# An encoder layer's up projection: one 512-column matmul in place of two of 256 in five of its seven products, with PSUM in pairs of banks

## The chip, the core and the metric

The kernel runs on one core of one Trainium2 chip. The metric is the device time of one execution in microseconds (us), the median of several runs. Engines are named as in the profile: PE is TensorE's matmul, PEld its weight load, DVE is VectorE, ACT is ScalarE, POOL is GpSimd, SP is SyncE. PSUM is the memory that PE writes; it has eight banks of 512 float32 values in each of 128 partitions.

## The reference

One layer of a streaming encoder on 512 tokens of width 2048, all in float32:

```python
h = rms_norm(x, pre_mix_g)
z = h @ w_in                        # q, k, v, u
a = chunked_attention(q, k, v, rel_bias)
p = multiscale_pool(u, pool_w, pool_scale)
x = x + rms_norm(concat([a, p]) @ w_o, post_mix_g)
h = rms_norm(x, pre_ffn_g)
up = causal_dwconv(h @ w_up, conv_w, conv_b)          # 2048 -> 2 * 5632, 3 taps
y = (gelu(up[..., :5632]) * up[..., 5632:]) @ w_down
x = x + rms_norm(y, post_ffn_g)
```

The change touches only `h @ w_up`.

## The kernel before

**Products in three parts.** A float32 factor is split into a high part, rounded to the type that PE multiplies in one pass, and a low part, the rest. ACT writes the high part (L135), DVE the low part (L136). A product of two split factors is three matmuls that add up in PSUM: `mm3` (L150 to L153) issues high by high (L151), high by low (L152) and low by high (L153).

**The up projection.** The columns of `w_up` are taken in 44 blocks k of 256 (two times 128), and each block's product with h is made by Winograd's form of Strassen's scheme: seven half-size products, numbered 1 to 7, in place of eight. One product (k, i) is 1024 deep and 256 tokens wide: `seven` (L853) runs over eight slices `kb` of 128 and issues three matmuls for each, 24 in all. The stationary operand is a 128x128 piece of w's factor (tiles `wfh` and `wfl`), the moving operand 256 columns of h's factor i, whose high and low part lie beside each other in one tile (`gT` for factors 1, 2, 5 and 3, `h` for 7, 4 and 6).

**The results of a block.** Products 1 and 2 share one PSUM bank (`q12`, half a bank each), 5 and 7 another (`q57`), 3 and 4 a third (`q34`), 6 has its own (`q6`). `half_bank` (L815) takes the bank that has been free longest from the list `spare`, and `done_bank` gives it back. `keep_six` (L829) follows product 6: ACT copies product 1 out (L844), DVE adds 6, 5 and 7, and 2 to it in the SBUF tile z (L845 to L850). `keep_all` (L1077) follows product 3: DVE adds both halves of `q34` into z in one instruction (L1080), and then the three taps of the convolution run on z (`taps`: ACT L1052, DVE L1053 and L1054), for an even block with the gelu (`gate`), for an odd one with the product of the two (`product`, DVE L1070). The tile z has two buffers.

**The order.** PE's order is the program's; the other engines' order is chosen by a scheduler. `Factors.order` (L700 to L712) lists the products. From block 5 to 42 a block's row is (k, 4), (k, 1), (k, 2), (k-1, 6), (k, 5), (k, 7), (k-1, 3): product 3 of a block ends the row of the next block, and product 4 of the block after that follows at once. Blocks 2 and 3 go together, and their last products (2, 6), (3, 6), (2, 3), (3, 3) stand directly before (4, 4). `Factors.get` splits each factor four products ahead; its tiles are those of the product that has just ended, so ACT's split waits for PE there.

After the up projection the down projection runs (`p` tiles, matmuls of 512 columns).

Of the kernel before, what the change touches and what calls it, by code (L numbers as in the profile page):

```python
# [9 lines left out]
F32 = mybir.dt.float32  # L10
F32R = mybir.dt.float32r
AF = mybir.ActivationFunctionType
# [3 lines left out]
P = 128  # L16
S = 512
# [11 lines left out]
WARM = 9  # L29
NU = KF // 2  # L30
EARLY = 5
CU = 4
AHEAD = 3
T = S // 2
# [42 lines left out]
def encoder_layer(ctx: ExitStack, tc: tile.TileContext, x, xT, vecs, rel, post_mix, post_ffn,  # L77
# [7 lines left out]
    nc = tc.nc  # L85
# [5 lines left out]
    mixing = ctx.enter_context(ExitStack())  # L91
    acc = mixing.enter_context(tc.tile_pool(name="acc", bufs=1))
    psum = ctx.enter_context(tc.tile_pool(name="psum", bufs=1, space=bass.MemoryType.PSUM))
    dram = ctx.enter_context(tc.tile_pool(name="dram", bufs=1, space=bass.MemoryType.DRAM))

    cycle = list(range(8))

    def bank(name, at=None):
        if at is None:
            at = cycle.pop(0)  # L100
            cycle.append(at)
        return psum.tile([P, 512], F32, tag=f"ps{at}", bufs=1, name=name)

    def acc8(name, which, dt=F32):
        return acc.tile([P, 2048], dt, tag="acc" + which, bufs=2, name=name)
# [44 lines left out]
    def mm3(ps, l, r, first, last):  # L150
        nc.tensor.matmul(ps, l[0], r[0], start=first, stop=False)  # L151
        nc.tensor.matmul(ps, l[0], r[1], start=False, stop=False)  # L152
        nc.tensor.matmul(ps, l[1], r[0], start=False, stop=last)  # L153
# [8 lines left out]
    def part(w, *idx):  # L162
        return tuple(v[(slice(None),) + idx] for v in w)
# [34 lines left out]
    for h in range(1, HEADS):  # L198
        q, k = qk_specs(h)
# [51 lines left out]
    for kb in range(KD):  # L251
        i, o = divmod(kb, 8)
        nc.sync.dma_start(xt[kb // 4][:, kb % 4, :], xT[kb * P:(kb + 1) * P, :])
        for what in "qk":
            if kb in chunks:
                raw, hi, lo = first[f"{what}0_{i}"]
# [5 lines left out]
        for what in "qk":  # L262
            _, hi, lo = first[f"{what}0_{i}"]
# [13 lines left out]
    with tc.tile_pool(name="p1", bufs=2, reuse_waits="tile") as p1:  # L277
# [209 lines left out]
        for g in range(4):  # L487
            hi, lo = (v[g].rearrange("p (a b) -> p a b", a=2) for v in (first_h, first_l))
# [32 lines left out]
        def at(f, kb, sl=slice(None)):  # L521
            return tuple(f[kb // 4][:, half, kb % 4, sl] for half in range(2))
# [56 lines left out]

    NC = (NU - 2) // CU  # L580
    H, C = S // 2, D // 2
    gd = [[dram.tile([P, CU, 2, H], F32, name=f"gd{c}_{i}") for i in range(2)] for c in range(NC)]
    gd_last = [dram.tile([P, 2, S], F32, name=f"gd{u}") for u in (NU - 2, NU - 1)]
# [109 lines left out]
    class Factors:  # L693
# [3 lines left out]
        def __init__(self):  # L697
            n = 2 * NU

            self.order = [(k, i) for k in range(EARLY) for i in (1, 2)]  # L700
            self.order += [(0, 5), (0, 7), (1, 5), (0, 6), (1, 7), (1, 6), (0, 3), (1, 3), (0, 4), (1, 4)]
            self.order += [(j, i) for i in (4, 7, 5, 6, 3) for j in (2, 3)]
            for k in range(EARLY - 1, n):
                late = [(k - 1, 6), (k - 1, 3)]
                if k < EARLY:
                    o = [(k, 4), (k, 7), (k, 5)]
# [6 lines left out]
            self.last = n - 1  # L713
            self.alone = *range(EARLY), n - 1
            self.raw, self.made, self.loaded, self.used = {}, [], 0, 0
# [6 lines left out]
        def source(self, k, i):  # L722
# [5 lines left out]
            if i == 7:  # L728
                return "v" if k < EARLY else "y"
            return "w" if i == 4 and k in self.alone else "x"  # L730
# [31 lines left out]
        def make(self, k, i):  # L762
            early, what = k < EARLY, self.source(k, i)
            v = self.raw[k, what]
# [41 lines left out]
    def flat(v):  # L806
        return v.rearrange("p a b -> p (a b)")

    p3, factors = None, Factors()
    banks, gates, zs, spare = {}, {}, {}, []  # L810

    def raw_x(name):
        return p3.tile([P, 1024], F32, tag="x", bufs=3, name=name)
# [1 line left out]
    def half_bank(k, i):  # L815
        tag = {5: "57", 7: "57", 1: "12", 2: "12", 6: "6", 3: "34", 4: "34"}[i]
        if (k, i) == (3, 6):
            return banks[2, "6"][0], slice(T, S)
        if (k, tag) not in banks:
            n = spare.pop(0)  # L820
            banks[k, tag] = bank(f"q{tag}_{k}", n), n
        return banks[k, tag][0], slice(T, S) if i in (7, 2, 4) else slice(0, T)

    def done_bank(k, tag):
        ps, n = banks.pop((k, tag))
        spare.append(n)
        return ps

    def keep_six(k, z=None):  # L829

        z = flat(new_z()) if z is None else z
        if k == 0:
            factors.held["r"].append((k, "six"))
            factors.raw[k, "six"] = z
        if k == 3:
            q6 = done_bank(2, "6")[:, T:]
        elif k == 2:
            q6 = banks[2, "6"][0]
        else:
            q6 = done_bank(k, "6")  # L840
        q57, q12 = (done_bank(k, n) for n in ("57", "12"))
        v2 = z[:, 3 * T:]
        for v in (v2, z[:, :T]):
            nc.scalar.activation(v, q12[:, :T], AF.Copy)  # L844
        nc.vector.tensor_add(v2, q6[:, :T], v2)  # L845
        nc.vector.tensor_add(z[:, T:3 * T].rearrange("p (a b) -> p a b", a=2),
                             q57.rearrange("p (a b) -> p a b", a=2),
                             v2[:, None, :].to_broadcast([P, 2, T]))
        nc.vector.tensor_add(v2, q57[:, :T], z[:, 2 * T:3 * T])
        nc.vector.tensor_add(z[:, :T], q12[:, T:], z[:, :T])  # L850
        zs[k] = z

    def seven(k, i):  # L853
        w = factors.get()
        ps, half = half_bank(k, i)
        for kb in range(8):
            mm3(ps[:, half], part(w, kb), at(h_f[i], kb), kb == 0, kb == 7)

    m = [None] * NT
    for i, tag in ((7, "raw1"), (4, "wh")):  # L860
# [8 lines left out]
    with tc.tile_pool(name="p2", bufs=1, reuse_waits="tile") as p2:  # L869
# [113 lines left out]
        for n in (5, 3):  # L983
            B = new_banks(f"m{n}", 4 if n == 5 else 0)
            for cc in range(2):
                late = (lambda q: h0.append(next(turning))) if n == 3 else None
                h0, ps = [], [B[cc, t] for t in range(2)]
# [17 lines left out]
        h_f = {1: gT[0][0], 2: gT[0][1], 5: gT[1][0], 3: gT[1][1]}  # L1005
        spare = [4, 5, 6, 7, 3]
# [8 lines left out]
        spare = [0, 1, 2]  # L1015
# [31 lines left out]
    p3 = phase.enter_context(tc.tile_pool(name="p3", bufs=2, reuse_waits="tile"))  # L1047
# [8 lines left out]
    def new_z():  # L1056
        return p3.tile([P, 2, S], F32, tag="z", name="z")
# [19 lines left out]
    def keep_all(k):  # L1077
        z = zs.pop(k)
        factors.raw.pop((k, "six"), None)
        nc.vector.tensor_add(z[:, T:3 * T], done_bank(k, "34"), z[:, T:3 * T])  # L1080
        z = z.rearrange("p (a b) -> p a b", a=2)
        u = k // 2
        if k % 2:
            product(u, gates.pop(u), z)
        else:
            gates[u] = gate(u, z)
# [28 lines left out]
    def next_first():  # L1115
# [2 lines left out]
        r = rights[0].send(i)  # L1118
        firsts.append((i, next(lefts), r))

    for k, i in rest:
        seven(k, i)
        if (k, i) == (end - 1, 3):
            next_first()
        if (k, i) == (2, 6):
            continue
        if i == 6:
            if k == 3:
                keep_six(2)
            keep_six(k)  # L1130
            if k == end:
                next_first()
        if i == (4 if k < 2 else 3):
            keep_all(k)
    cycle[:] = spare
    firsts = [(i, multiply(l, r)) for i, l, r in firsts]
    phase.close()

# [244 lines left out]
```

## Time and profile before

| | |
|---|---|
| median of 3 runs | 1920.13 us (1920.1 to 1920.24) |
| the profiled execution | 1921.21 us, of it span 1919.4 us |
| PE busy | 1890.6 us, 11898 matmuls |
| DVE busy | 1416.2 us |
| ACT busy | 949.9 us |
| granted TensorE clock, mean | 0.991 |

Times in the trace count from the start of the span. The attention and the output projection fill the span up to about 590 us, the up projection goes from there to about 1460 us, and the down projection takes the rest. A matmul's duration in the profile holds the time that its results take to drain, so those of neighbours overlap: the pace is the distance from start to start, or a stretch divided by the matmuls in it. A row of the timeline has start, duration, engine, line and tiles (written <- read), and in brackets how long the engine sat idle before it and for whom. A row of the windows has the stretch, its length, busy time with the number of instructions of each engine asked for, the granted clock as a share of full speed, the share of DMA and GB/s.

### The profile page before, as it was taken

How to read it: one execution, taken by the hardware profiler on the slowest of the kernel's cores; microseconds unless marked ns; L12 is line 12 of the kernel's file. 1: busy time of each engine (PE TensorE's matmuls, PEld its weight loads, DVE VectorE, ACT ScalarE, POOL GpSimd, SP SyncE). 2: the span in 40 equal slices, each digit the busy share in tenths (PEclk: the TensorE clock that was granted, in tenths of full speed). 3: DMA queues.
4: the chain of work that ended last, by engine and by line, in shares of the span. 5: the costliest groups of instructions: out<-in, count | busy, mean ns of one | idle time of the engine just before them, and what ended most of it. 6: DMA issues, size and time to landing. Idle time of an engine off the chain costs nothing.

```text
span 1919.4 us, 29449 instructions
## 1 busy us (share of the span) xinstructions
PE 1890.6 (98%) x11898; PEld 1719.5 (90%) x11898; DVE 1416.2 (74%) x1626; ACT 949.9 (49%) x1178; POOL 290.6 (15%) x383
## 2 busy tenths in 40 slices
PE   9999999999998999999999999999999899999998
PEld 7888888888888999999999999999998688888887
DVE  5554345686688677777777777777778899998877
ACT  6333233355487455445444454544545555565543
POOL 5000000000011121111111111111110112222211
PEclk9999999999999999999999999999999899999999
DMA  9747947667877876776766767667676779999998
GB/s 330 213 120 170 247 115 203 156 186 228 285 279 200 213 170 150 182 181 152 187 157 170 188 150 187 164 159 189 158 183 192 259 209 261 250 221 248 220 226 242
DMA packets 175529, 383.81 MB, mean 200 GB/s; under 512 B 11041, under 2 KB 62625, under 8 KB 172833
## 3 DMA queue, kind: packets, MB, share of 16 engines
q0 software_dynamic: 45472, 137.38, 38.5%
q1 hardware_dynamic: 129920, 244.55, 37.6%
q8 instruction: 93, 1.52, 0.3%
q14 instruction: 44, 0.35, 0.1%
HBM read 325.27 MB, written 90.18 MB: 216 GB/s over the span
## 4 chain that ended last, share of the span: by engine, by line
PE 92%; DVE 4%; DMA 2%; issue 1%; ACT 1%; SPq 0%; POOL 0%; POOLq 0%; DVEq 0%; ACTq 0%
PE q L153 16%; PE q L151 16%; PE q L152 16%; PE p L153 6%; PE p L152 6%; PE p L151 6%; PE m L152 2%; PE m L151 2%; PE m L153 2%; PE u L151 2%; PE v L152 2%; PE u L152 2%; PE v L151 2%; PE u L153 2%; PE v L153 2%; PE k L152 1%
## 5 line engine op out<-in xcount | busy, mean ns | idle before, releaser
L151 PE MATMUL q<-gT,wfh 128*128 128x256 f32 x1392 | 394.4, 283 | 0.0
L152 PE MATMUL q<-gT,wfh 128*128 128x256 f32 x1392 | 394.2, 283 | 0.0
L153 PE MATMUL q<-gT,wfl 128*128 128x256 f32 x1392 | 394.1, 283 | 0.0
L151 PE MATMUL q<-h,wfh 128*128 128x256 f32 x1056 | 300.7, 285 | 8.5 <-DVE z L845 7.2
L152 PE MATMUL q<-h,wfh 128*128 128x256 f32 x1056 | 300.6, 285 | 1.4 <-DVE h L136 1.4
L153 PE MATMUL q<-h,wfl 128*128 128x256 f32 x1056 | 300.7, 285 | 0.8 <-DVE wfl L136 0.8
L135 ACT ACTIVATE wfh<-wx 128x1024 fp32r<-128x1024 f32 x171 | 181.3, 1060 | 192.0 <-PE q L152 142.4
L152 PEld LDWEIGHTS q<-gT,wfh 128*128 128x128 f32 x1392 | 267.5, 192 | 0.2 <-DVE gT L136 0.2
L151 PEld LDWEIGHTS q<-gT,wfh 128*128 128x128 f32 x1392 | 267.5, 192 | 0.0
L153 PEld LDWEIGHTS q<-gT,wfl 128*128 128x128 f32 x1392 | 267.4, 192 | 0.0
L136 DVE TENSOR_TENSOR wfl<-wx,wfh 128x1024 fp32r<-128x1024 f32 x171 | 208.7, 1222 | 66.0 <-ACT wfh L135 65.8
L152 PE MATMUL p<-bl,ah 128*128 128x512 f32 x560 | 220.4, 394 | 4.4 <-DVE bl L136 4.4
L153 PE MATMUL p<-bh,al 128*128 128x512 f32 x560 | 220.4, 394 | 2.1 <-DVE al L136 2.1
L151 PE MATMUL p<-bh,ah 128*128 128x512 f32 x560 | 220.2, 393 | 1.8 <-ACT ah L135 1.8
L151 PEld LDWEIGHTS q<-h,wfh 128*128 128x128 f32 x1056 | 204.5, 194 | 8.9 <-DVE z L845 7.4
L152 PEld LDWEIGHTS q<-h,wfh 128*128 128x128 f32 x1056 | 204.4, 194 | 1.8 <-DVE h L136 1.8
L153 PEld LDWEIGHTS q<-h,wfl 128*128 128x128 f32 x1056 | 204.5, 194 | 1.0 <-DVE wfl L136 1.0
L135 ACT ACTIVATE bh<-b 128x2048 fp32r<-128x2048 f32 x70 | 133.3, 1915 | 76.8 <-DVE b L629 44.0
L136 DVE TENSOR_TENSOR bl<-b,bh 128x2048 fp32r<-128x2048 f32 x70 | 159.0, 2287 | 11.9 <-PE p L152 6.0
L760 POOL DMA_DIRECT2D wx<-in_w_up x90 | 79.6, 888 | 519.5 <-DVE wfl L136 440.6
L135 ACT ACTIVATE wfh<-wy 128x1024 fp32r<-128x1024 f32 x82 | 86.6, 1057 | 107.8 <-PE q L152 107.5
L136 DVE TENSOR_TENSOR wfl<-wy,wfh 128x1024 fp32r<-128x1024 f32 x82 | 100.3, 1223 | 48.4 <-ACT wfh L135 48.4
(417 smaller groups left out, 3729.6 us busy)
## 6 DMA issues: line engine op xcount, KB each, us to landing
wx<-in_w_up POOLq DMA_DIRECT2D x90, 512.0 KB, 6.3
b<-in_w_down SPq DMA_DIRECT2D x42, 1024.0 KB, 7.8
sum<-part POOLq DMA_DIRECT2D x70, 512.0 KB, 8.3
wx<-in_w_up SPq DMA_DIRECT2D x45, 512.0 KB, 5.9
wy<-in_w_up SPq DMA_DIRECT2D x44, 512.0 KB, 6.5
wz<-in_w_up SPq DMA_DIRECT2D x44, 512.0 KB, 5.2
wy<-in_w_up POOLq DMA_DIRECT2D x39, 512.0 KB, 6.1
wo_sum<-in_w_o POOLq DMA_DIRECT2D x16, 1024.0 KB, 11.2
```

The costliest lines, as they stand in the source:

```text
L135: rounded = nc.scalar.activation(hi, src, AF.Copy)
L136: nc.vector.tensor_sub(lo, src, f32(hi))
L151: nc.tensor.matmul(ps, l[0], r[0], start=first, stop=False)
L152: nc.tensor.matmul(ps, l[0], r[1], start=False, stop=False)
L153: nc.tensor.matmul(ps, l[1], r[0], start=False, stop=last)
L760: nc.gpsimd.dma_start(self.raw[k, what], self.block(k, m, kh), accum_op=ALU.add)
```

## The change

From block 4 on (`PAIRED = 4`), products 3 to 7 no longer use `mm3`. For each `kb` there is one matmul of w's high part with 512 moving columns, both parts of h's factor at once (now L910), which fills a whole bank: high by high in the first 256 columns, high by low in the last 256. A second matmul adds w's low part by h's high part to the first half (L909 for the last `kb`, where it goes ahead, else L912). So a product has 16 matmuls instead of 24, and its result is the sum of the two halves of its bank, which DVE has to add. Products 1 and 2 stay as they were.

A product then needs a whole bank. From (4, 4) on, PSUM holds bank 0 for `q12`, bank 1 for `q6`, and three pairs of banks: one pair for products 5 and 7, and two for 3 and 4, of which block k takes number `k % 2`. Nothing is taken from `spare` any more.

The steps behind the products become: `begin_z` (after product 2: an ACT copy L843 and a DVE add L844), `keep_pair` (after 5 and 7: an ACT copy L849 of 512 values into a tile t57, and a DVE add L850 of the other halves), `finish_six` (after 6: two DVE adds L856 from PSUM, and L857 and L859 within SBUF), and in `keep_all` two DVE adds L1140 of 512 values where there was one. For block 4 `begin_z` stands before the product (4, 4), since its `q12` lies in a bank that the pairs take.

```diff
+PAIRED = EARLY - 1
...
-            n = spare.pop(0)
+            n = k - 2 if tag == "34" and k in (2, 3) else spare[0]
+            spare.remove(n)
...
+    def pair_bank(k, i):
+        tag = "57" if i in (5, 7) else "34"
+        if (k, tag) not in banks:
+            n = 2 if tag == "57" else k % 2
+            banks[k, tag] = pairs.tile([P, 2, S], F32, tag=f"pair{n}", bufs=1, name=f"q{tag}_{k}")
+        return banks[k, tag][:, int(i in (7, 4)), :]
+
+    def begin_z(k):
+        z = zs[k] = flat(new_z())
+        q12 = banks.pop((k, "12"))[0]
+        nc.scalar.activation(z[:, 3 * T:], q12[:, :T], AF.Copy)
+        nc.vector.tensor_add(z[:, :T], q12[:, T:], z[:, 3 * T:])
+
+    def keep_pair(k):
+        q57 = banks.pop((k, "57"))
+        t57[k] = v = p3.tile([P, 2, T], F32, tag="t", bufs=1, name="t57")
+        nc.scalar.activation(v, q57[:, :, :T], AF.Copy)
+        nc.vector.tensor_add(v, q57[:, :, T:], v)
+
+    def finish_six(k):
+        z, q6, t = zs[k], banks.pop((k, "6")), t57.pop(k)
+        v2 = z[:, 3 * T:]
+        for half in range(2):
+            nc.vector.tensor_add(v2, q6[:, half * T:(half + 1) * T], v2)
+        nc.vector.tensor_add(z[:, T:3 * T].rearrange("p (a b) -> p a b", a=2), t,
+                             v2[:, None, :].to_broadcast([P, 2, T]))
+        nc.vector.tensor_add(v2, t[:, 0, :], z[:, 2 * T:3 * T])
...
         for kb in range(8):
-            mm3(ps[:, half], part(w, kb), at(h_f[i], kb), kb == 0, kb == 7)
+            hi, lo = part(w, kb)
+            if kb == 7:
+                nc.tensor.matmul(ps[:, :T], lo, at(h_f[i], kb)[0], start=False, stop=False)
+            nc.tensor.matmul(ps.rearrange("p (a b) -> p a b", a=2), hi, both(h_f[i], kb), start=kb == 0, stop=kb == 7)
+            if kb < 7:
+                nc.tensor.matmul(ps[:, :T], lo, at(h_f[i], kb)[0], start=False, stop=False)
...
-        nc.vector.tensor_add(z[:, T:3 * T], done_bank(k, "34"), z[:, T:3 * T])
+        if k < PAIRED:
+            nc.vector.tensor_add(z[:, T:3 * T], done_bank(k, "34"), z[:, T:3 * T])
+        else:
+            q34, v = banks.pop((k, "34")), z[:, T:3 * T].rearrange("p (a b) -> p a b", a=2)
+            for half in range(2):
+                nc.vector.tensor_add(v, q34[:, :, half * T:(half + 1) * T], v)
...
     for k, i in rest:
+        if k == PAIRED and pairs is None:
+            begin_z(k)
+            singles.close()
+            pairs = up_banks.enter_context(
+                tc.tile_pool(name="pairs", bufs=1, space=bass.MemoryType.PSUM, reuse_waits="tile"))
         seven(k, i)
```

How the order moves, at three places. First PE, at the seam of two rows of the list: the end of product 3 of block 18 and the start of product 4 of block 20 (`q34_18` and `q34_20` are the PSUM tiles of products 3 and 4 of these blocks; brackets name the engines whose counters the matmul waits on). Before:

```order
L151 MATMUL q34_18_8905<-gT11_4767,wfh_9190 128x256
L152 MATMUL q34_18_8905<-gT11_4767,wfh_9190 128x256
L153 MATMUL q34_18_8905<-gT11_4767,wfl_9191 128x256
L151 MATMUL q34_20_9361<-h40_5119,wfh_9218 128x256 [waits Activation_49]
L152 MATMUL q34_20_9361<-h40_5119,wfh_9218 128x256
L153 MATMUL q34_20_9361<-h40_5119,wfl_9219 128x256 [waits DVE_49]
```

Now:

```order
L910 MATMUL q34_18_8426<-gT11_4770,wfh_8667 128x512
L912 MATMUL q34_18_8426<-gT11_4770,wfl_8668 128x256
L909 MATMUL q34_18_8426<-gT11_4770,wfl_8668 128x256
L910 MATMUL q34_18_8426<-gT11_4770,wfh_8667 128x512
L910 MATMUL q34_20_8810<-h40_5122,wfh_8698 128x512 [waits DVE_49,PE_49,Activation_49]
L912 MATMUL q34_20_8810<-h40_5122,wfl_8699 128x256
```

Before, the first matmul of (20, 4) waits for its factor alone: ACT's high part on L151, DVE's low part on L153. Now it also waits, on DVE, for the second L1140 of block 18, which reads both banks of the pair that `q34_20` takes over.

Second DVE, at the same seam (`wfl` are splits of later factors, `z` the sums of block 18). Before:

```order
L136 TENSOR_TENSOR wfl_9258<-wy_9057,wfh_9257 128x1024 [waits DMAHW5_49,PE_49,Activation_49]
L136 TENSOR_TENSOR wfl_9290<-wz_9087,wfh_9289 128x1024 [waits DMAHW7_49,PE_49,Activation_49]
L1080 TENSOR_TENSOR z_9248<-q34_18_8905,z_9248 128x512 [waits DVE_49,PE_49]
L136 TENSOR_TENSOR wfl_9320<-wx_8799,wfh_9319 128x1024 [waits DMASW7_49,Activation_49]
L1053 SCALAR_TENSOR_TENSOR ca_9348<-z_9248,vec_71,ca_9348 128x511 [waits DMASW6_49,DMASW5_49,Activation_49]
```

Now:

```order
L144 TENSOR_TENSOR wfl_8727<-wy_8554,wfh_8726 128x1024 [waits DMAHW5_49,PE_49,Activation_49]
L144 TENSOR_TENSOR wfl_8751<-wz_8579,wfh_8750 128x1024 [waits DMAHW7_49,PE_49,Activation_49]
L850 TENSOR_TENSOR t57_8770<-q57_19_8731,t57_8770 128x512 [waits Activation_49]
L1140 TENSOR_TENSOR z_8501<-q34_18_8426,z_8501 128x512 [waits PE_49]
L1140 TENSOR_TENSOR z_8501<-q34_18_8426,z_8501 128x512 [waits DVE_49]
L144 TENSOR_TENSOR wfl_8776<-wx_8340,wfh_8775 128x1024 [waits DMASW7_49,Activation_49]
```

The addition of products 5 and 7 of block 19 (L850) has come in ahead of the two L1140, of which the second waits for the first.

Third DVE, around the last products of blocks 2 and 3, ahead of (4, 4) (`z_5758`, now `z_5761`, belongs to block 3). Before:

```order
L1080 TENSOR_TENSOR z_5758<-q34_3_5544,z_5758 128x512
L136 TENSOR_TENSOR wfl_5848<-wy_5637,wfh_5847 128x1024 [waits DMAHW1_49,PE_49,Activation_49]
L1053 SCALAR_TENSOR_TENSOR cb_5833<-z_5758,vec_71,cb_5833 128x511 [waits Activation_49]
L1053 SCALAR_TENSOR_TENSOR cb_5838<-z_5758,vec_71,cb_5838 128x511 [waits Activation_49]
L1054 SCALAR_TENSOR_TENSOR cb_5833<-z_5758,vec_71,cb_5833 128x510 [waits DVE_49]
L1054 SCALAR_TENSOR_TENSOR cb_5838<-z_5758,vec_71,cb_5838 128x510 [waits DVE_49]
L1070 TENSOR_TENSOR ca_5795<-ca_5795,cb_5833 128x512 [waits DVE_49]
L1070 TENSOR_TENSOR ca_5795<-ca_5795,cb_5838 128x512 [waits DVE_49]
```

Now:

```order
L1136 TENSOR_TENSOR z_5761<-q34_3_5547,z_5761 128x512
L1108 SCALAR_TENSOR_TENSOR cb_5836<-z_5761,vec_74,cb_5836 128x511 [waits Activation_49]
L1108 SCALAR_TENSOR_TENSOR cb_5841<-z_5761,vec_74,cb_5841 128x511 [waits Activation_49]
L1109 SCALAR_TENSOR_TENSOR cb_5836<-z_5761,vec_74,cb_5836 128x510 [waits DVE_49]
L1109 SCALAR_TENSOR_TENSOR cb_5841<-z_5761,vec_74,cb_5841 128x510 [waits DVE_49]
L1125 TENSOR_TENSOR ca_5798<-ca_5798,cb_5836 128x512 [waits DVE_49]
L1125 TENSOR_TENSOR ca_5798<-ca_5798,cb_5841 128x512 [waits DVE_49]
L844 TENSOR_TENSOR z_5848<-q12_4_5041,z_5848 128x256 [waits Activation_49]
```

`begin_z(4)` (L844) now stands behind the whole convolution of block 3, and the first matmul of (4, 4) waits for it; before, that matmul waited for L849 of block 2, which stands ahead of all these rows.

More of the change, by code (lines that the diff above doesn't have):

```diff
@@ L93, in encoder_layer, with upper @@
     psum = ctx.enter_context(tc.tile_pool(name="psum", bufs=1, space=bass.MemoryType.PSUM))
+    singles = ctx.enter_context(ExitStack())
+    def upper(name, stack):
+        return stack.enter_context(tc.tile_pool(name=name, bufs=1, space=bass.MemoryType.PSUM, reuse_waits="tile"))
+    upper_pool = upper("psb", singles)
     dram = ctx.enter_context(tc.tile_pool(name="dram", bufs=1, space=bass.MemoryType.DRAM))
@@ L101, in bank @@
             cycle.append(at)
-        return psum.tile([P, 512], F32, tag=f"ps{at}", bufs=1, name=name)
+        pool = psum if at < 2 else upper_pool
+        return pool.tile([P, 512], F32, tag=f"ps{at}", bufs=1, name=name)
     def acc8(name, which, dt=F32):
@@ L809, in encoder_layer @@
     p3, factors = None, Factors()
-    banks, gates, zs, spare = {}, {}, {}, []
+    banks, gates, zs, t57, spare, pairs = {}, {}, {}, {}, [], None
     def raw_x(name):
@@ L851, in keep_six, with both @@
         zs[k] = z
+    def both(f, kb):
+        return f[kb // 4][:, :, kb % 4, :]
     def seven(k, i):
         w = factors.get()
-        ps, half = half_bank(k, i)
-        for kb in range(8):
-            mm3(ps[:, half], part(w, kb), at(h_f[i], kb), kb == 0, kb == 7)
+        if k < PAIRED or i < 3:
+            if k > PAIRED and (k, "12") not in banks:
+                banks[k, "12"] = bank(f"q12_{k}", 0), 0
+            ps, half = half_bank(k, i)
+            for kb in range(8):
+                mm3(ps[:, half], part(w, kb), at(h_f[i], kb), kb == 0, kb == 7)
+            return
+        if i == 6:
+            ps = banks[k, "6"] = bank(f"q6_{k}", 1)
+        else:
+            ps = pair_bank(k, i)
+        for kb in range(8):
+            hi, lo = part(w, kb)
[4 more added lines that the diff above has]
+                nc.tensor.matmul(ps[:, :T], lo, at(h_f[i], kb)[0], start=False, stop=False)
     m = [None] * NT
@@ L1079, in keep_all @@
         factors.raw.pop((k, "six"), None)
-        nc.vector.tensor_add(z[:, T:3 * T], done_bank(k, "34"), z[:, T:3 * T])
+        if k < PAIRED:
+            nc.vector.tensor_add(z[:, T:3 * T], done_bank(k, "34"), z[:, T:3 * T])
+        else:
+            q34, v = banks.pop((k, "34")), z[:, T:3 * T].rearrange("p (a b) -> p a b", a=2)
+            for half in range(2):
+                nc.vector.tensor_add(v, q34[:, :, half * T:(half + 1) * T], v)
         z = z.rearrange("p (a b) -> p a b", a=2)
@@ L1119, in next_first @@
         firsts.append((i, next(lefts), r))
+    up_banks, done = ctx.enter_context(ExitStack()), {}
     for k, i in rest:
-        seven(k, i)
+        if k == PAIRED and pairs is None:
[3 more added lines that the diff above has]
+                tc.tile_pool(name="pairs", bufs=1, space=bass.MemoryType.PSUM, reuse_waits="tile"))
+        seven(k, i)
+        if k > PAIRED and i == 2:
+            begin_z(k)
+        done.setdefault(k, set()).add(i)
+        if k >= PAIRED and i in (5, 7) and {5, 7} <= done[k]:
+            keep_pair(k)
         if (k, i) == (end - 1, 3):
@@ L1129, in encoder_layer @@
                 keep_six(2)
-            keep_six(k)
+            if k < PAIRED:
+                keep_six(k)
+            else:
+                finish_six(k)
             if k == end:
@@ L1134, in encoder_layer @@
             keep_all(k)
-    cycle[:] = spare
+    up_banks.close()
+    upper_pool = upper("psb", ctx)
+    for n in range(2, 8):
+        bank("place", n)
+    cycle[:] = 4, 5, 0, 2, 3, 1, 6, 7
     firsts = [(i, multiply(l, r)) for i, l, r in firsts]
```

## The prediction

> **What bounds the kernel now.** I read the page's totals and its chain first, then the costliest groups, then windows and the timeline of the up projection.
>
> ```profile
> span 1919.4 us, 29449 instructions
> PE 1890.6 (98%) x11898; PEld 1719.5 (90%) x11898; DVE 1416.2 (74%) x1626; ACT 949.9 (49%) x1178; POOL 290.6 (15%) x383
> ...
> PE 92%; DVE 4%; DMA 2%; issue 1%; ACT 1%; SPq 0%; POOL 0%; POOLq 0%; DVEq 0%; ACTq 0%
> ...
> L151 PE MATMUL q<-h,wfh 128*128 128x256 f32 x1056 | 300.7, 285 | 8.5 <-DVE z L845 7.2
> ```
>
> PE is busy for 98% of the span and carries 92% of the chain, and the matmuls of the up projection hardly ever wait: of the group shown, 8.5 us in 1056. So PE's pace sets the time. It can be read from two stretches without a gap, one in the up projection (256 columns), one in the down projection (512 columns); the number behind x counts matmuls:
>
> ```profile
> 700.00:1400.00 700.00, 700.00 (x5836) 1.00 0.69 171
> ...
> 1700.00:1800.00 100.00, 100.00 (x443) 1.00 0.99 234
> ```
>
> 700/5836 is 119.9 ns for 256 columns, 100/443 is 225.7 ns for 512. Two of 256 cost 2 x 119.9 - 225.7 = 14.1 ns more than one of 512: that much of a matmul does not depend on its columns. Work behind PE has room:
>
> ```profile
> 900.00:1000.00 100.00, 100.00 (x836) 100.00 (x835) 74.40 (x89) 50.00 (x58) 16.10 (x19) 1.00 0.69 169
> ...
> DVE z L1080 <- PE q L153: 24.1, 37, 0.7
> ```
>
> In the first row DVE (third figure) is busy for 74 of 100 us. The second, from the table of waits of the up projection, says that DVE stands idle for PE 37 times, 0.65 us each, before it adds products 3 and 4: it is ready there when PE ends product 3.
>
> **Part 1, fewer matmuls.** Blocks 4 to 43 have 5 products with 8 pairs of matmuls that become one: 40 x 5 x 8 = 1600. At 14.1 ns each that is 1600 x 0.0141 = 22.6 us less, all of it on PE and so on the path. The bounds: nothing, if a matmul of 256 behind one of 512 cannot keep its pace, and twice that, 45 us, if the narrow one behind the wide one sheds its own 14.1 ns too; the trace has matmuls of 256, 384 and 512 in a row, and they keep their paces:
>
> ```profile
> 300.34 0.39 PE L153 MATMUL a<-pth,vl 128*128 128x512 f32 x1
> 300.57 0.33 PE L151 MATMUL a<-pth,vh 128*128 128x384 f32 x1
> ...
> 301.22 0.28 PE L152 MATMUL a<-ptl,vh 128*128 128x256 f32 x1
> 301.34 0.29 PE L153 MATMUL a<-pth,vl 128*128 128x256 f32 x1
> ```
>
> 0.23 us from the one of 512 to the next, 0.12 between those of 256. I take 22.6.
>
> The Trainium skill has a smaller price here: its page "TensorE: Matmul & The Clock Gate", section "Wait — 56ns, not 53.3ns?", gives a fixed cost of about 2.5 ns to each warm matmul, by which this part would save an estimated 4 us and the sum below would be some 19 us higher; the trace's 14.1 ns decides.
>
> **Part 2, a wait at every seam of the list.** Blocks k and k + 2 share one pair of banks, and (k+2, 4) follows (k, 3) directly. So PE stops until DVE has run both L1140, which themselves wait for (k, 3). Today PE runs on at this place:
>
> ```profile
> 1001.64 0.28 PE L153 MATMUL q<-gT,wfl 128*128 128x256 f32 x1
> ...
> 1001.76 0.28 PE L151 MATMUL q<-h,wfh 128*128 128x256 f32 x1
> ...
> 1001.84 1.06 ACT L135 ACTIVATE wfh<-wx 128x1024 fp32r<-128x1024 f32 x1 [1.82 <-PE q L152]
> ...
> 1001.96 0.69 DVE L1080 TENSOR_TENSOR z<-q,z 128x512 f32<-128x512 f32 x1 [0.68 <-PE q L153]
> ```
>
> Product 3 ends with the matmul at 1001.64, product 4 of the block after next starts at 1001.76, and DVE starts its addition 0.04 us after the drained end (1001.64 + 0.28). Then the rows for two additions in a chain, and for PE held by DVE:
>
> ```profile
> 1013.68 0.42 DVE L845 TENSOR_TENSOR z<-q,z 128x256 f32<-128x256 f32 x1
> 1014.14 0.69 DVE L846 TENSOR_TENSOR z<-q,z 128x512 f32<-128x512 f32 x1
> ...
> 620.22 0.42 DVE L845 TENSOR_TENSOR z<-q,z 128x256 f32<-128x256 f32 x1
> ...
> 620.69 0.58 PE L151 MATMUL q<-h,wfh 128*128 128x256 f32 x1 [7.16 <-DVE z L845]
> ...
> 1497.75 0.39 PE L153 MATMUL p<-bh,al 128*128 128x512 f32 x1
> ...
> 1499.97 0.50 PE L151 MATMUL p<-bh,ah 128*128 128x512 f32 x1 [1.83 <-ACT ah L135]
> ...
> 1500.31 0.40 PE L152 MATMUL p<-bl,ah 128*128 128x512 f32 x1
> ```
>
> L846 needs L845's result and starts 0.04 us after its end. PE starts 0.05 us after the DVE instruction that held it (620.22 + 0.42 to 620.69). The first matmul behind a wait takes 0.34 us to the next, not 0.226, since its weights are loaded only then: 0.11 more. From the start of the last 512-column matmul of (k, 3): 0.39 to its drained end, 0.04, 0.69, 0.04, 0.69, 0.05, in all 1.90 us to the next start, where 0.226 would do. One seam costs 1.90 - 0.226 + 0.11 = 1.78 us. Seams of this kind stand ahead of (6, 4) to (42, 4), that is 37; at (43, 4) product (43, 5) lies between and hides it. 37 x 1.78 = 65.9 us.
>
> Is DVE there in time? Ahead of the two L1140 it now also has L850, which waits for ACT's copy and stands behind the split of z's factor:
>
> ```profile
> 998.88 0.28 PE L151 MATMUL q<-gT,wfh 128*128 128x256 f32 x1
> ...
> 998.96 1.06 ACT L135 ACTIVATE wfh<-wz 128x1024 fp32r<-128x1024 f32 x1 [1.77 <-PE q L152]
> ...
> 1000.05 1.23 DVE L136 TENSOR_TENSOR wfl<-wz,wfh 128x1024 fp32r<-128x1024 f32 x1 [1.60 <-ACT wfh L135]
> ```
>
> The split ends 2.4 us after product 3's start (998.88), L850 takes another 0.7 at most: 3.1. Product 3 will last 8 x (0.2257 + 0.1199) = 2.76, and 0.16 more until it has drained: 2.93, plus 0.04. DVE's instructions overlap by some 0.08 us in the timeline, so it is about level. A seam is thus 1.78 us, perhaps 0.2 more, and hardly less than 1.5 (were the second addition to overlap the first by 0.3).
>
> The other new additions (L856, L857, L859, L844) hide behind later products: banks 0 and 1 and the pair of 5 and 7 are wanted again only five or more products, over 13 us, later (at the very end, at (43, 5), one product later: a few tenths, once). DVE's 15.0 us of a block (74.4% of 168 x 0.1199 = 20.1) grow by L850, the second L1140 (0.69 each) and the second L856 (0.42, as L845) to 16.8: no bound.
>
> **Part 3, the clock.** A gap can also cost clock. Rows around gaps (stretch, length, PE busy, granted clock), each pair on neighbouring stretches:
>
> ```profile
> 606.31:609.72 3.41, 2.31 (x19) 1.00 0.28 112
> 609.72:613.13 3.41, 3.41 (x30) 1.00 0.96 150
> 654.10:657.51 3.41, 1.70 (x12) 1.00 0.92 179
> 657.51:660.92 3.41, 3.06 (x14) 0.50 0.20 50
> 1497.18:1500.59 3.41, 1.58 (x7) 1.00 0.49 197
> 1500.59:1504.01 3.42, 1.90 (x5) 0.50 0.47 133
> ...
> 1487.16 0.63 PE L152 MATMUL p<-bl,ah 128*128 128x512 f32 x1
> 1487.59 0.63 PE L153 MATMUL p<-bh,al 128*128 128x512 f32 x1
> ```
>
> The clock changes on a grid of 3.41 us. A stretch with 2.31 us of busy PE kept it, stretches with 1.70 and 1.58 were followed by one at half clock, where the pace is 0.43 us instead of 0.226. A seam leaves PE idle for 1.90 - 0.39 = 1.51 us, so a stretch that holds all of it is busy for 1.90: nearer to 1.70 than to 2.31. I take it as lost. A seam falls whole into one stretch in (3.41 - 1.51)/3.41 = 56% of the cases. One stretch at half clock loses 3.41 x (1 - 0.226/0.43) = 1.6 us. 37 x 0.56 x 1.6 = 33 us, between 0 and, were 1.2 us of idle enough, 37 x 0.74 x 1.6 = 44.
>
> **Part 4, the entry.** (4, 4) waits for L844 of block 4, behind the convolution of block 3:
>
> ```profile
> 670.56 0.28 PE L151 MATMUL q<-h,wfh 128*128 128x256 f32 x1
> ...
> 675.52 0.69 DVE L1080 TENSOR_TENSOR z<-q,z 128x512 f32<-128x512 f32 x1
> ...
> 680.20 1.29 DVE L1070 TENSOR_TENSOR ca<-ca,cb 128x512 f32<-128x512 f32 x2
> ...
> L850 DVE TENSOR_TENSOR z<-q,z 128x256 f32<-128x256 f32 x44 | 18.5, 421 | 0.0
> ```
>
> Today (4, 4) starts at 670.56, and the last L1070 of block 3 ends at 680.20 + 1.29 = 681.49. With 0.3 to 0.42 for L844 and 0.05, PE starts at about 681.8: 11.2 us late, plus about 2 us of half clock behind so long a gap, 13 in all (5 to 15, if DVE gets through earlier).
>
> **The sum**, against the profiled execution's 1921.2 us (span 1919.4 and 1.8 around it; 1.1 over the median): 1921.2 - 22.6 + 65.9 + 33 + 13 = 2010.5, against the median 2009.
>
> **The rivals.**
>
> *The clock holds.* Busy for 1.90 of 3.41 us is a case that the trace does not have, and the threshold may lie below it. Then Part 3 falls away but for the entry: 2010.5 - 33 - 1.1 = 1976 us. For it speaks that 2.31 kept the clock and that the gap at 1497.75 was longer, 1.83; against it the nearer row. The Trainium skill's page "TensorE: Matmul & The Clock Gate" speaks on both sides: "What's actually happening" has the clock fall after an idle window of about 3.4 us, which no seam reaches, while "A second HAM failure mode: psum-queue depth-cycling" tells of clocks that oscillate from short gaps between groups of matmuls that cycle through PSUM banks. The trace contradicts the first (1.83 us of waiting was enough at 1497.75).
>
> *DVE becomes the bound at the seam.* If L850 is late, because ACT's copy queues behind its splits, both L1140 slip. From 0.1 us of lateness on each tenth costs 37 x 0.1 = 3.7 us; 0.5 us, half a split, would give 18 us and make the loss of clock surer: about 2030.
>
> *Faster: the seam costs less than the matmuls save.* The place is the same first matmul of (k+2, 4). If its wait were over when PE gets there, Part 1 alone would remain with the entry: 1921.2 - 22.6 + 13 - 1.1 = 1910. It decides at 22.6/37 = 0.6 us per seam (less with the entry); but one L1140 alone is 0.69, and both start only after (k, 3). Hence a small chance.
>
> *The matmuls save nothing*, for the reason in Part 1: 23 us on top of the first sum or of the rival's, 2032 or 1999.
>
> **How the numbers follow.** The forecast (seams and lost clock) 0.5; the clock holds 0.33; DVE late 0.08; nothing saved 0.04; seams cheaper than the saving 0.05, of which 0.02 for those that only make it level. The range takes in both likely cases, with 1.6 us instead of 1.78 at a seam below the second (1976 - 7 = 1969, taken as 1968) and 44 for 33 and some lateness above the first (2009 + 11 + 5 = 2025). It leaves out the faster case and about half of the two dear ones, and tails, near 2 in 10. Differences under 0.2% (3.8 us) count as none, as a measurement of this kernel can hardly tell them. Slower by more than that holds in all cases but the last: 0.95; faster 0.03, same 0.02.
>
> **What would show it.** In the profile after: 37 waits of PE on DVE's L1140 of about 1.5 us each, and one of about 11 us on L844 at about 670; some 1.6 thousand fewer matmuls; the pair of a 512 and a 256 matmul at 346 ns where three took 360; half-clock stretches behind about 20 of the seams, a mean clock near 0.97 (21 x 3.41 us at half, 1.8% of the span, under today's 0.99). It would be wrong if the waits are much under 1 us, if they last over 2 (DVE late), or if the clock in the up projection stays at 1.00 (then about 1976).

## The result and the profile after

The changed kernel takes 1995.05 us (1994.02 to 1995.5, 4 runs) against 1920.18 before: 1.0387 times as long, 95% interval 1.0375 to 1.0399. It is slower by 75 us. The forecast was 2009 and the rival in which the clock holds stood at 1976: the time lies between the two. The profiled execution took 1994.02 us.

The page's totals after, and its costliest group:

```profile
span 1992.2 us, 26429 instructions
PE 1888.5 (95%) x10298; PEld 1634.4 (82%) x10298; DVE 1487.3 (75%) x1746; ACT 959.4 (48%) x1178; POOL 290.6 (15%) x383
...
L910 PE MATMUL q<-h,wfh 128*128 128x512 f32 x960 | 354.1, 403 | 71.8 <-DVE z L1140 59.2
```

1600 matmuls are gone (11898 to 10298), but PE's busy time has hardly moved (1890.6 to 1888.5) and the span has grown by 72.8 us. The last figures of the third row say where to look: PE was idle for 71.8 us ahead of the first wide matmuls of products that read `h`, and 59.2 of it ended with DVE's L1140. The table of PE's waits (engine, what it issued, what it waited for: us in total, times, longest) splits the 71.8 into its two causes:

```profile
PE q L910 <- DVE z L1140: 59.2, 37, 1.6
PE q L910 <- DVE z L844: 12.6, 1, 12.6
```

37 seams of 1.60 us and one entry of 12.6. The timeline of one seam, at the place where PE ran on before:

```profile
1014.78 0.69 DVE L850 TENSOR_TENSOR t<-q,t 128x512 f32<-128x512 f32 x1
...
1015.17 0.39 PE L910 MATMUL q<-gT,wfh 128*128 128x512 f32 x1
...
1015.60 1.42 DVE L1140 TENSOR_TENSOR z<-q,z 128x512 f32<-128x512 f32 x2
...
1017.16 0.47 PE L910 MATMUL q<-h,wfh 128*128 128x512 f32 x1 [1.60 <-DVE z L1140]
...
1017.47 0.28 PE L912 MATMUL q<-h,wfl 128*128 128x256 f32 x1
```

Product 3's last matmul drains at 1015.17 + 0.39 = 1015.56, DVE starts 0.04 later, adds twice in 1.42 us, and PE starts 0.14 us after that. L850, whose lateness was a rival, ends at 1015.47, before product 3 does. From the last start to the next it is 1.99 us, and all seams are alike: the first of a regular row and the thirty-sixth after it are

```profile
711.65 0.39 PE L910 MATMUL q<-gT,wfh 128*128 128x512 f32 x1
...
1492.20 0.39 PE L910 MATMUL q<-gT,wfh 128*128 128x512 f32 x1
```

(1492.20 - 711.65) / 36 = 21.68 us for a block, where the 168 matmuls of before took 168 x 0.1199 = 20.14.

The clock did not fall at any seam. The long window, and a stretch of the clock's grid that holds a whole seam with the one behind it (stretch, length, PE busy with matmuls, granted clock, share of DMA, GB/s):

```profile
700.00:1400.00 700.00, 648.79 (x4135) 1.00 0.67 158
...
754.67:758.08 3.41, 1.81 (x10) 1.00 0.73 137
758.08:761.50 3.42, 3.42 (x26) 1.00 0.00 0
```

PE was busy for 1.81 of 3.41 us, less than the 1.90 of the forecast, and the next stretch has full clock.

### The profile page after: what moved, and what is told of

Same layout as the page of the kernel before. It is cut to its first block, busy times and chain, and to the rows that moved or that the text cites. A ratio compares the mean times of both kernels' runs of the same rounds, so it can differ in the third digit from the quotient of the medians.

```text
span 1992.2 us, 26429 instructions
## 1 busy us (share of the span) xinstructions
PE 1888.5 (95%) x10298; PEld 1634.4 (82%) x10298; DVE 1487.3 (75%) x1746; ACT 959.4 (48%) x1178; POOL 290.6 (15%) x383
## 5 line engine op out<-in xcount | busy, mean ns | idle before, releaser
L910 PE MATMUL q<-h,wfh 128*128 128x512 f32 x960 | 354.1, 403 | 71.8 <-DVE z L1140 59.2
L910 PEld LDWEIGHTS q<-h,wfh 128*128 128x128 f32 x960 | 181.8, 190 | 115.8 <-ACT wfh L143 69.9
L912 PE MATMUL q<-h,wfl 128*128 128x256 f32 x840 | 237.0, 282 | 0.0
L910 PE MATMUL q<-gT,wfh 128*128 128x512 f32 x640 | 232.0, 397 | 0.0
L159 PE MATMUL q<-gT,wfh 128*128 128x256 f32 x752 | 213.3, 284 | 0.0
L160 PE MATMUL q<-gT,wfh 128*128 128x256 f32 x752 | 213.3, 284 | 0.0
L161 PE MATMUL q<-gT,wfl 128*128 128x256 f32 x752 | 213.2, 284 | 0.0
L912 PEld LDWEIGHTS q<-h,wfl 128*128 128x128 f32 x840 | 160.0, 190 | 1.9
L912 PE MATMUL q<-gT,wfl 128*128 128x256 f32 x560 | 157.2, 281 | 0.0
L160 PEld LDWEIGHTS q<-gT,wfh 128*128 128x128 f32 x752 | 142.5, 190 | 1.9 <-DVE gT L144 0.2
L159 PEld LDWEIGHTS q<-gT,wfh 128*128 128x128 f32 x752 | 142.6, 190 | 0.0
L161 PEld LDWEIGHTS q<-gT,wfl 128*128 128x128 f32 x752 | 142.5, 190 | 0.0
L910 PEld LDWEIGHTS q<-gT,wfh 128*128 128x128 f32 x640 | 120.5, 188 | 21.8 <-DVE t L850 0.3
```

The costliest lines, as they stand in the source:

```text
L910: nc.tensor.matmul(ps.rearrange("p (a b) -> p a b", a=2), hi, both(h_f[i], kb), start=kb == 0, stop=kb == 7)
L912: nc.tensor.matmul(ps[:, :T], lo, at(h_f[i], kb)[0], start=False, stop=False)
```

## The experiments

All times are medians beside runs of the kernel before on the same chip (1920.01 to 1920.06 us there). Ratios are to the kernel before.

**One product between the seam's two.** Product 4 goes behind product 1, so that the additions of L1140 have a whole product's time:

```diff
-                    o = [(k, 4), (k, 1), (k, 2), late[0], (k, 5), (k, 7), late[1]]
+                    o = [(k, 1), (k, 4), (k, 2), late[0], (k, 5), (k, 7), late[1]]
```

> The changed kernel with product 1 of a block ahead of its product 4 in the list, so that one product lies between (k, 3) and (k+2, 4). Theory (the seam's wait on both L1140 is a cost of its own, 37 times 1.99 - 0.235 + 0.07 = 1.83 us): the 37 waits of PE on L1140 are gone, since a product of 256-column matmuls lasts 2.87 us and the wait 1.76; 1995 - 68 = 1927 us. Rival (the wait only moves: bank 0 of products 1 and 2 is freed one product later than it is wanted, or DVE falls behind): PE waits on L844 or on later L1140 instead, and the time stays above 1960 us.

1933.1 us (1931.88 to 1935.94), ratio 1.0072 [1.0057, 1.0087], 6 us above what was expected. PE's waits:

```profile
PE q L910 <- DVE z L844: 12.3, 1, 12.3
...
PE q L910 <- DVE t L850: 4.5, 1, 4.5
```

No wait on the two additions is left, and the time has fallen by 62 us (1995.05 to 1933.1). The entry stays. A new wait of 4.5 us on L850 stands at the very end of the up projection; it is most of the 6 us that were not expected.

**The factor's two parts in one piece.** In the changed kernel the 512 moving columns are two pieces of 256 that lie 1024 or 2048 values apart. Here they lie side by side:

```diff
-        return [hold(tag, f"{name}{i}").rearrange("p a b -> p (a b)").rearrange("p (s a b) -> p s a b", s=2, a=4)
+        return [hold(tag, f"{name}{i}").rearrange("p a b -> p (a b)").rearrange("p (a s b) -> p s a b", s=2, a=4)
```

and the tiles of factor 3 in the same way.

> The changed kernel with high and low part of each 128-row slice of h's factors side by side in SBUF, so that the 512 moving columns are one run of 512 instead of two of 256 that lie apart. Theory (the wide matmul's pace of 0.235 to 0.24 us instead of 0.226 comes from the two pieces): the pace falls to 0.226, 1600 x 0.009 = 14 us less, 1981 us. Rival (it comes from filling a whole bank, or from standing between narrow matmuls): pace and time stay, 1995 us. The waits at the seams stay at 1.60 us each in both.

1996.37 us (1994.89 to 1997.72), ratio 1.0399 [1.0384, 1.0415]: no gain. The pace is what it was:

```profile
999.92 0.40 PE L910 MATMUL q<-h,wfh 128*128 128x512 f32 x1
1000.16 0.28 PE L912 MATMUL q<-h,wfl 128*128 128x256 f32 x1
1000.28 0.40 PE L910 MATMUL q<-h,wfh 128*128 128x512 f32 x1
1000.52 0.28 PE L912 MATMUL q<-h,wfl 128*128 128x256 f32 x1
```

0.24 us behind the wide one and 0.12 behind the narrow one. That theory falls.

**The entry.** Other banks for the first blocks, so that (4, 4) finds a free pair and does not wait for block 4's `begin_z`:

```diff
-            n = k - 2 if tag == "34" and k in (2, 3) else spare[0]
+            n = {2: 5, 3: 1}[k] if tag == "34" and k in (2, 3) else spare[0]
...
-        spare = [4, 5, 6, 7, 3]
-        turning = turned(1, xn, 0)
+        spare = [4, 5, 6, 7, 0]
+        turning = turned(1, xn, 1)
...
-        spare = [0, 1, 2]
+        spare = [1, 2, 3]
```

> The changed kernel with other banks before the pairs begin: products 1 and 2 of block 4 in bank 0, which no pair takes, so that (4, 4) no longer waits for L844; product 1 of block 5, four products later, does. Theory (the entry costs its wait of 12.6 us and some 5 us of half clock behind it): both go, 1995 - 15 = 1980 us, and the seams stay. Rival (DVE's backlog behind blocks 2 and 3 is the cause, and PE meets it a little later in any case): a wait of over 5 us appears at one of the next products, time above 1987 us.

1980.11 us (1977.87 to 1980.5), ratio 1.0315 [1.0298, 1.0333]: 14.9 us less than the changed kernel, as expected, with the seams' row of the waits word for word as it was (59.2, 37, 1.6) and none on L844.

**All three together.**

> The three edits together: product 1 ahead of 4, the parts side by side, and the banks at the entry. Theory (three separate costs that add up): 1995 - 68 - 14 - 15 = 1898 us, 1% under the kernel before, which has none of the three and lacks only the saving of 1600 matmuls at 14 ns. Rival (they hide one another, or DVE becomes the bound once PE no longer stops): 1910 to 1930 us, with waits of PE on DVE spread over the up projection.

1923.64 us (1920.2 to 1924.68), ratio 1.0019 [1.0009, 1.0028]. 26 us above what was expected. 14 of them are the pace, which the second edit did not change, and 6 what the first edit alone had already fallen short by. Two waits remain, the first at the end of the up projection (at 1441.72), the second at the entry (at 681.46), which is not quite free in this order:

```profile
PE q L910 <- DVE t L850: 5.0, 1, 5.0
...
PE q L159 <- DVE z L844: 2.7, 1, 2.7
```

**Another order.** Instead of moving product 4, product 3 of the block before goes ahead of product 7, so that 7 stands at the seam. The entry is mended as above, the factor's layout is the changed kernel's:

```diff
-                    o = [(k, 5), (k, 4), (k, 1), (k, 2), late[0], (k, 7), late[1]]
+                    o = [(k, 4), (k, 5), (k, 1), (k, 2), late[0], (k, 7), late[1]]
...
-                    o = [(k, 4), (k, 1), (k, 2), late[0], (k, 5), (k, 7), late[1]]
+                    o = [(k, 4), (k, 1), (k, 2), late[0], (k, 5), late[1], (k, 7)]
```

> Banks at the entry as in e3_entry, and product 3 of the block before one place earlier, ahead of product 7 instead of behind it, so that product 7 lies between (k, 3) and (k+2, 4) while products 4, 1, 2 and the transfers that hang on them keep their places; in the last row 4 goes ahead of 5. Theory (e1_order gave back 6 of its 68 us because product 4 and its transfer moved, which made PE wait 4.5 us at the end for L850 behind a late wx): no wait of PE on DVE in the up projection longer than 1 us, its end at about 1460 in the trace, and in all 1920 - 12 (1600 pairs at 0.352 us instead of 0.360) + 1 + up to 4 in the down projection = 1909 to 1913 us, faster than the kernel before. Rival (the pairs of banks cost a wait wherever product 3 stands): 1920 us or more, with waits on L850 or L1140.

1923.99 us (1923.0 to 1925.86), ratio 1.0025 [1.0014, 1.0035], 11 us above the upper end of what was expected. The seams are free (of their waits one of 0.4 us is left), and at the end of the up projection stands a long wait:

```profile
1435.30 1.06 ACT L143 ACTIVATE wfh<-wx 128x1024 fp32r<-128x1024 f32 x1 [8.45 <-DMA wx<-in_w_up]
...
1439.08 0.62 PE L910 MATMUL q<-h,wfh 128*128 128x512 f32 x1 [4.64 <-DVE z L1140]
```

ACT's split waits 8.45 us for a transfer of w, DVE's work behind it comes late, and PE waits for that, and 2.0 us more on L850 soon after.

**Wide ones first, narrow ones after.** If it is the change from a wide to a narrow matmul that costs, a product should be faster with one such change in place of eight. The same kernel, with its 16 matmuls grouped:

```diff
         for kb in range(8):
             hi, lo = part(w, kb)
-            if kb == 7:
-                nc.tensor.matmul(ps[:, :T], lo, at(h_f[i], kb)[0], start=False, stop=False)
-            nc.tensor.matmul(ps.rearrange("p (a b) -> p a b", a=2), hi, both(h_f[i], kb), start=kb == 0, stop=kb == 7)
-            if kb < 7:
-                nc.tensor.matmul(ps[:, :T], lo, at(h_f[i], kb)[0], start=False, stop=False)
+            nc.tensor.matmul(ps.rearrange("p (a b) -> p a b", a=2), hi, both(h_f[i], kb), start=kb == 0, stop=False)
+        for kb in range(8):
+            hi, lo = part(w, kb)
+            nc.tensor.matmul(ps[:, :T], lo, at(h_f[i], kb)[0], start=False, stop=kb == 7)
```

> e5_three with the eight wide matmuls of a product first and its eight narrow ones behind them, instead of in turns. Theory (in turns a pair takes 0.352 us where the down projection's wide matmuls take 0.2257 and narrow ones 0.1199, together 0.3456: the change of width costs 6 ns): in groups 0.2257 and 0.1199, another 1600 x 0.0065 = 10 us under e5_three. Rival (a matmul whose 512 columns hold both parts takes 0.235 us wherever it stands): 0.235 among wide ones, 0.120 among narrow ones, and the time of e5_three or up to 5 us over it.

1918.9 us (1917.01 to 1921.03, 11 runs), ratio 0.9997 [0.9988, 1.0006], 5.1 us less than the ungrouped one, half of the 10 that were expected. The timeline joins equal matmuls that follow each other:

```profile
914.45 2.00 PE L908 MATMUL q<-gT,wfh 128*128 128x512 f32 x8
916.29 1.12 PE L911 MATMUL q<-gT,wfl 128*128 128x256 f32 x8
917.25 2.00 PE L908 MATMUL q<-h,wfh 128*128 128x512 f32 x8
```

A product takes 917.25 - 914.45 = 2.80 us. 8 wide ones take 1.84 us, 0.230 each, 8 narrow ones 0.96, 0.12 each. In the changed kernel the pair takes 0.352, a product 2.82. So changing to and fro costs about 0.02 to 0.025 us a product; 200 of them are 4 to 5 us, and that is the measured difference. The trace's single starts show it within the group: 0.234 and 0.235 for the first two wide ones, 0.227 for the last three. So the wide ones come down to the pace of the forecast only late in their group.

**The narrow one into the other half of the bank.** It might be that the narrow matmul is slowed by following the wide one into the same columns:

```diff
-                nc.tensor.matmul(ps[:, :T], lo, at(h_f[i], kb)[0], start=False, stop=False)
+                nc.tensor.matmul(ps[:, T:], lo, at(h_f[i], kb)[0], start=False, stop=False)
```

> e5_three with the low part's matmul adding into the second half of the bank instead of the first (the sum of the halves is the same). Theory (the pace has nothing to do with which columns are written): paces of 0.235 and 0.117 us and the time of e5_three within 2 us. Rival (the narrow matmul and the next wide one are held up because they add to columns just written): the pair falls towards 0.346 us, up to 10 us under e5_three.

1923.43 us (1921.28 to 1924.87, 11 runs), ratio 1.002 [1.0011, 1.0028], with the paces as before (0.235 and 0.117). The columns are not the cause.

**A longer seam.** The changed kernel, with a copy of 128 columns by DVE behind the two additions, for which the seam then waits too. Does the clock fall at more than 1.60 us?

```diff
+            nc.vector.tensor_copy(early[:, :128], q34[:, 0, :128])
```

> The changed kernel with one more DVE instruction behind the two L1140, which copies 128 columns of the pair out and which (k+2, 4) has to wait for too: about 0.33 us more at each of the 37 seams, PE idle for 1.93 us instead of 1.60. Theory (the clock holds as long as a stretch of 3.41 us of the grid has over about 1.75 us of busy PE: 1.70 lost it in the kernel before, 1.81 kept it in the changed one): stretches with 1.48 us of busy PE lose it, behind some 60% of the seams; 1995 + 12 + 35 = 2042 us. Rival (single gaps of under 2 us never cost clock; the lost stretches before had other causes): 2007 us at full clock.

2106.99 us (2106.62 to 2107.24), ratio 1.098 [1.0965, 1.0995]: 112 us above the changed kernel, 65 more than expected. The waits and DVE's rows at one seam say half of it:

```profile
PE q L910 <- DVE early L1141: 108.5, 37, 2.9
...
1007.88 1.42 DVE L1140 TENSOR_TENSOR z<-q,z 128x512 f32<-128x512 f32 x2
1009.21 1.22 DVE L144 TENSOR_TENSOR wfl<-wx,wfh 128x1024 fp32r<-128x1024 f32 x1
1010.34 0.28 DVE L1141 COPY early<-q 128x128 f32<-128x128 f32 x1
```

The scheduler put a split of 1.22 us between the additions and the copy, so PE waited 2.93 us and not 1.9: (2.93 - 1.60) x 37 = 49 us. The rest, 63, is clock: nearly every seam was followed by one or two stretches at half clock. This settles that seams can lose the clock, but not from which length.

**The threshold.** To lengthen the wait without another instruction, the second addition takes 640 or 768 columns (it then also adds into columns of z that are not its own, so these two kernels do not compute the layer):

```diff
-            for half in range(2):
-                nc.vector.tensor_add(v, q34[:, :, half * T:(half + 1) * T], v)
+            nc.vector.tensor_add(v, q34[:, :, :T], v)
+            nc.vector.tensor_add(z[:, T:T + 640], q34.rearrange("p a b -> p (a b)")[:, 1024 - 640:], z[:, T:T + 640])
```

> The changed kernel with the second L1140 at each seam taking 640 columns of the pair of banks instead of 512, into the wrong columns of z (the sums are no longer those of the reference). PE's idle time at a seam should go from 1.60 to about 1.74 us, since a DVE instruction of 256 columns took 0.42 and one of 512 took 0.69. Threshold theory: the clock is halved for a stretch of 3.41 us behind each stretch in which PE was busy for 1.70 us or less, and kept at 1.81 or more; a stretch that holds a whole seam now has 1.67. 37 x 0.14 = 5 us for the longer wait, and between 19 and 31 seams x 1.7 us for the clock (half of the seams if they fall on the grid by chance, more if a lost stretch brings the next seam back to the same place of the grid): 2030 to 2050 us. Rival, a threshold well below 1.67 us of busy time (the kernel with 2.93 us of idle time at a seam is still explained): 1995 + 5 = 2000 us, no stretch of half clock at the seams.

> As the kernel with 640 columns, with 768: idle time at a seam about 1.87 us, busy time in a stretch that holds a whole seam about 1.54. Threshold theory: 37 x 0.27 = 10 us for the wait, and between 20 and 33 seams x 1.7 us for the clock: 2040 to 2061 us. Rival, a threshold below 1.54 us of busy time: 2005 us without stretches of half clock at the seams. If 640 keeps the clock and 768 loses it, the threshold lies between 1.54 and 1.67.

640 columns: 2000.03 us (1996.42 to 2000.71), ratio 1.0411 [1.0396, 1.0425]. 768 columns: 2047.45 us (2047.05 to 2048.24), ratio 1.0662 [1.0647, 1.0676]. The threshold theory as put missed the first, where its rival (2000) came true, and hit the second. The waits with 640, and a stretch that holds a seam with the one behind it:

```profile
PE q L910 <- DVE z L1140: 64.1, 37, 1.7
...
711.43:714.84 3.41, 1.68 (x10) 1.00 0.89 155
714.84:718.26 3.42, 3.42 (x23) 1.00 0.02 5
```

And with 768:

```profile
PE q L910 <- DVE z L1140: 69.1, 37, 1.9
...
711.73:715.14 3.41, 1.54 (x10) 1.00 0.86 154
715.14:718.56 3.42, 3.42 (x11) 0.50 0.02 5
```

0.14 us more of waiting per seam (64.1 / 37 = 1.73 to 69.1 / 37 = 1.87) is 5 us for 37 seams, but the time rises by 47. With 1.73 no seam lost the clock, though 19 stretches of the grid had PE busy for 1.68 to 1.70 us only. With 1.87, 29 of the 30 stretches with 1.54 or 1.55 us were followed by one at half clock; those with 1.59 and more were not. The 29 cost (47.4 - 5) / 29 = 1.46 us each.

Busy time alone does not part lost from kept: the kernel before lost the clock behind a stretch with 1.70 us, the one with 640 columns kept it with 1.68. The rows of the former show a difference:

```profile
655.01 0.28 PE L153 MATMUL q<-gT,wfl 128*128 128x256 f32 x1
656.59 0.38 PE L151 MATMUL q<-h,wfh 128*128 128x256 f32 x1 [1.30 <-ACT wfh L135]
656.82 0.28 PE L152 MATMUL q<-h,wfh 128*128 128x256 f32 x1
```

The stretch from 654.10 to 657.51 holds the ends of two runs of matmuls, and the busy time holds the drain of both, 0.16 us each. With the last matmul of each run counted by its pace (0.12 us), PE was at work from 654.10 to 655.13 and from 656.59 to 656.94, in all 1.38 us. Counted in this way, an estimate from the starts and paces of the traces, the full-clock stretches from 592 to 1860 us fall in order in five traces (before, changed, the copy, 640 and 768 columns): all with 1.50 or less were followed by half clock (1.38 in 27 of the 29 with 768 columns), all with 1.51 or more were not (1.51 to 1.53 for most seams with 640 columns that lie whole in a stretch, 1.65 for most of the changed kernel). Other traces have exceptions: with product 4 behind product 1 a stretch of 1.35 kept the clock (at 1444.29), with all three edits together one of 1.64 lost it (at 655.16). So this count is nearer than the busy time, but not exact either.

**The end mended.** The grouped version, with the last two rows of the list put back:

```diff
+                elif k == n - 2:
+                    o = [(k, 4), (k, 1), (k, 2), late[0], (k, 5), (k, 7), late[1]]
```

and (k, 5) ahead of (k, 4) again in the last row.

> The grouped version (8 wide matmuls, then 8 narrow; order 4, 1, 2, 6, 5, 3, 7) with the last two rows of the list put back as in the changed kernel. Theory: the waits at the end of the up projection there (4.56 us on L1139 at 1434 to 1439, 0.99 us on L850, and a stretch of half clock that made the 8 wide matmuls behind take 3.25 us and cost about 1.4 more) come from the order of these two rows. They go: 1918.9 - 4.6 - 1.0 - 1.4 = about 1912 us, ratio to before 0.996. Rival: ACT's split is held there by a late transfer of w into wx whatever the order is; then the wait moves to another product and the time stays at 1917 to 1920.

1911.43 us (1909.97 to 1914.03), ratio 0.9952 [0.9938, 0.9965], as expected: 0.5% faster than the kernel before. The waits on the additions, and a product:

```profile
PE q L910 <- DVE z L1141: 1.6, 1, 1.6
...
1009.36 2.00 PE L910 MATMUL q<-gT,wfh 128*128 128x512 f32 x8
1011.20 1.12 PE L913 MATMUL q<-gT,wfl 128*128 128x256 f32 x8
1012.15 2.00 PE L910 MATMUL q<-gT,wfh 128*128 128x512 f32 x8
```

One wait of 1.6 us on the additions is left, where a block early in the list meets its pair, and a product takes 2.79 us. The idea of the change is thus worth having: what it lacked was an order in which almost nothing waits for the two additions, banks for the entry, and equal matmuls side by side.

## Why the prediction was right or wrong, point by point

**Part 1 (-22.6 us): the mechanism was right, the size was not.** Fewer matmuls do save time, but a product takes 2.82 us against 24 x 0.1199 = 2.88 before: 0.058 x 200 = 11.5 us, half of what was forecast. The step that failed is the pace of the wide matmul. 0.2257 was read from a stretch that holds nothing but wide matmuls; behind a narrow one it is 0.235, and of the 9 ns too much the narrow one gives back 3. Grouped, the products come to 2.79 to 2.80 us, and about 16 of the 22.6 us are there. Why a wide matmul is slower behind a narrow one stays open: neither the layout of the moving operand nor the columns written made a difference. The row from the attention that was to show that a mix keeps its paces (0.23 to the next) was printed to 0.01 us, too coarse for 9 ns. The Trainium skill's fixed cost per matmul ("TensorE: Matmul & The Clock Gate", "Wait — 56ns, not 53.3ns?") gave an estimated 4 us of saving; the measured 11.5 lie between that and the forecast.

**Part 2 (+65.9): right, in mechanism and size.** 37 waits at the place named, 1.99 us from start to start in place of 1.90. The terms 0.39, 0.04 and 1.42 stand in the timeline as forecast; PE started 0.14 us after DVE's end, not 0.05. The first matmul takes 0.31 to the next, so a seam costs 1.99 - 0.235 + 0.075 = 1.83 us, not 1.78, and 37 of them 67.7. Taking them away by order alone gave back 62. DVE was in time, by 0.13 us in the rows above.

**Part 3 (+33): wrong, and the largest miss.** The step "nearer to 1.70 than to 2.31. I take it as lost" failed. Behind none of the 37 seams did the clock fall; the window from 700 to 1400 has it at 1.00, which the prediction had named as a sign of being wrong. Seams that leave PE 1.60 or 1.73 us idle keep the clock; with 1.87 most lose it. A distance of 0.2 us between two rows did not bear a forecast, and the row of 1.70 was not of the same kind: it holds two drains, a seam's stretch only one. Without drains the two stand at 1.38 and 1.65. Even then the trace of before had nothing between 1.38, which lost the clock, and 2.15 (the row of 2.31), which kept it; what would have been right is a range from both ends with an even chance, and the rival got 0.33. What exactly the clock goes by stays open. The rule of the Trainium skill that speaks against a loss ("TensorE: Matmul & The Clock Gate", "What's actually happening": the clock falls after an idle window of about 3.4 us) is not borne out: 1.87 us of idle time in a stretch of 3.41 was enough. The Trainium skill's "A second HAM failure mode: psum-queue depth-cycling" on the same page, where short idle times between groups of matmuls make the clock oscillate, is nearer to what the kernels with 1.87 and 2.93 us do, but gives no length.

**Part 4 (+13): right.** PE waited 12.6 us on L844 at the entry. Half clock lay over the start behind it (PE busy 5.42 of 14.50 us, granted clock 0.53):

```profile
672.00:686.50 14.50, 5.42 (x17) 0.53 0.51 108
```

Mending it gave 14.9 us.

**The sum.** Against the forecast the clock was 33 us cheaper; the saving was 11 smaller, the seams and the entry each 2 dearer. The down projection ran about 4 us longer (400.9 us from its first matmul to its last, 396.8 before): PE waits there 12.0 us for splits of its factors by ACT and DVE, 8.3 before. The change leaves its matmuls as they were but hands it the PSUM banks in another order; whether that is the cause was not tested. -33 + 11 + 2 + 2 + 4 = -14, and 2009 - 14 = 1995. That the forecast missed by 14 only is in part luck: a term that was 33 too high met others that were 19 too low together. The range held the time because it reached to the rival in which the clock holds, and that rival, not the forecast, had the clock right.

## What to carry to other kernels

Before a group of banks is made twice as wide, look at who reads it last and who writes it next: if these stand side by side in PE's order, every reuse shows DVE's whole chain of additions, and one product put between them gave 62 us of some 68 back. Price a merged matmul by its pace in the mix in which it will stand, not from a stretch of its own kind, and put equal sizes together. A small gap is not small where the clock changes: 0.14 us more at each of 37 seams cost 47 us here.

## What the runs showed that was not expected

- Between two seam lengths the clock's threshold is sharp: at 1.73 us of idle time none of 37 seams lost it, at 1.87 us 29 did.
- Losses feed on themselves. In the kernel with 768 columns the half-clock stretches begin mostly 23.9 us apart, which is 7 steps of 3.41. A block takes 21.9 us without a loss and 23.45 with one, 0.44 short of 7 steps, so the seam that follows a loss falls nearly on the same place of the grid and is lost too; after three or four one escapes. 29 of 37 seams were hit, where chance would have given about half. The Trainium skill's page "TensorE: Matmul & The Clock Gate", "What's actually happening", has the window run freely, without a reset when a kernel starts; this trace agrees in that all its stretches of half clock, from 616 to 2043 us, begin on one grid.
- The matmul that follows a wide one starts 0.235 us after it where wide and narrow take turns; from the sixth wide one in a row on it is 0.227.
- An edit to an order has its price at the list's end: two rows decided between 1918.9 and 1911.43 us. With the first, ACT waited 8.59 us for a transfer of w near the end of the up projection and PE behind it; with the second, 4.30 us there, and PE hardly waited (0.2 us).
